# Attention in a two-block kernel: full-height score products, and one chain of products with the values per pair of heads

## The chip, the cores and the metric

The program runs on one core of a Trainium2 chip. The metric is the device time of one execution in microseconds (us), the median over runs. Engines go by short names: PE is TensorE's matmul stream, PEld its weight loads, DVE is VectorE, ACT is ScalarE, POOL is GpSimd, SP is the queue that issues the weights' DMAs.

## The reference, cut to what matters

Two blocks over 512 tokens of 1024 features, in float32. The second block has two layers. Each mixes tokens by attention with 12 heads over the tokens and 4 heads over a memory of 256 tokens, 64 features a head, and has a gated feed forward behind it. Layer 0 is causal with a forget term, layer 1 a dilated attention that the kernel writes as one softmax with a table added to the scores.

```python
# layer 0, one block of 128 queries of a head
sc = jnp.einsum('bhqd,bhkd->bhqk', qi, k, preferred_element_type=jnp.float32) * scale
sc = sc + ci[..., :, None] - c[..., None, :]
sc = jnp.where(kpos[None, :] <= qpos[:, None], sc, NEG)
p = jax.nn.softmax(sc, axis=-1)
return jnp.einsum('bhqk,bhkd->bhqd', p.astype(v.dtype), v)
# memory, both layers
p = jax.nn.softmax(sc, axis=-1)
return jnp.einsum('bhqk,bhkd->bhqd', p.astype(vm.dtype), vm)
```

## The kernel before, in words

Activations lie by features, [128 features, 512 tokens]. A float32 product is made of exact halves: an operand is split into an upper part hi in the rounded format fp32r and the rest lo, and a projection (`proj`, `mm3`, line 174) is three products of 128x512 for each of eight tiles of the contraction: hi by hi, hi by lo, lo by hi. `wload` (lines 142 to 155) loads a weight slab, and splits it on ACT (L152) and DVE (L153).

A layer's attention is `_mix` (line 1405). It handles two pairs of memory heads (256 keys) and then six pairs of heads over the tokens. A pair has 64 + 64 features on the 128 partitions, head 0 on the partitions 0 to 63 and head 1 on 64 to 127; `H` names the two ranges. For a pair the projections give q and k (48 products of 128x512), `_stack_q` and `_stack_k` make the halves, and `_attend` (line 1295) does the rest. `_stack_q` puts a head's upper half of q on its own partitions and the lower half on the other 64, in one tile `sq` per head. `_stack_k` puts the upper half of k on both ranges (`skh`, one tile per head), and the lower half of both heads into one tile `skl`, each on its own range.

`_attend` goes through two halves of the queries, and in each through two heads and two blocks of 128 queries, eight score tiles in all. A score tile has w columns: 256 for the memory; for the tokens 256, 256, 384 and 512 as the causal range grows. It takes two products: L1311 with all 128 rows (upper q and lower q by upper k), L1312 with 64 rows (upper q by lower k). In layer 0 a third, bf16 product adds the causal mask (L1314). Then comes the softmax on DVE (L1318, or L1321 and L1322) and ACT (L1319 or L1323), a scale (L1326, L1328), transposes on PE (L1331), and copies into the tile `pt` (L1334, L1336). At the end of each half the products with the values (L1340) follow: 128 rows, 64 columns of weights, head 0 into the partitions 0 to 63 of `po` and head 1 into 64 to 127. Each is recorded as two matmuls, because the operands are plain float32. `po` is split (L161, L163) and goes into the output projection `w_out_2`.

The order of the instructions on each engine is set by a scheduler when the program is built; it interleaves the projections of a later pair with the attention of an earlier one. Within an engine the order is then fixed. The tags in `_layer` (line 1557) give the buffers: `st=8` for sq, skh and skl, `pt2=2`, `pt4=1`; in PSUM `mm=3`, `sm=2` for scores, `pT=2`, `po=1`.

Of the kernel before, what the change touches and what calls it, by code (L numbers as in the profile page):

```python
# [28 lines left out]
# k-tiles of the layers' down products, in the parts that follow one another  # L29
# [3 lines left out]
# columns of the table of per-feature vectors, [128, columns]  # L33
# [11 lines left out]
# column tiles of w_in, in the order in which they are used  # L45
A_ORDER = (6, 2, 0, 4, 3, 1, 5)
# the tile of them that the modulation's shift comes in after
SHIFT_AT = 5
# pieces of the merges before the recurrence, and for each of its stages
# [7 lines left out]
def _constants():  # L57
    """Arrays that depend on shapes alone."""
    c = {}
# [33 lines left out]
class _Core:  # L93
    """Pools, constants and the pieces that every stage uses."""
# [13 lines left out]
    # ---- tiles  # L108
    @contextmanager
    def tags(self, space=None, side=None, **n):  # L110
        """Within it g(), or ps(), takes tiles of each of these tags: n of them, 2 KB a partition each."""
# [29 lines left out]
    # ---- weights: exact halves of a slab [128, kt, cols]  # L141
    def wload(self, src, kt, cols, tag=None):
        """The halves stay in tiles of a tag if one is given."""
# [13 lines left out]
    def split(self, src, tag, scale=1.0, n=512):  # L157
        """Exact halves of scale * src; scale is a power of two or a column."""
# [10 lines left out]
    def mm3(self, out, w, x, first=True, last=True):  # L169
        """out += w.T @ x for operands in exact halves: lists over the tiles of the contraction."""  # L170
        n, total = 0, 3 * len(w)
        for (wh, wl), (xh, xl) in zip(w, x):
            for a, b in ((wh, xh), (wh, xl), (wl, xh)):
                self.nc.tensor.matmul(out, lhsT=a, rhs=b, start=first and n == 0, stop=last and n == total - 1)  # L174
                n += 1

    def proj(self, src, x, kt=8, name="mm", w=None):
        """One tile [128 columns, tokens] of a product with a slab of 128 columns."""
# [7 lines left out]
    # ---- numerics on small tiles  # L186
    def rsqrt(self, y, x, t):
        """y = x ** -0.5 to float32's accuracy, for x > 0."""
# [8 lines left out]
    def exp(self, out, x, pool, shape, tag):  # L197
        """out = exp(x) to float32's accuracy; x is overwritten."""
# [15 lines left out]
    def sincos(self, sn, cs, x, pool, shape, tag):  # L214
        """Sine and cosine to float32's accuracy; x is overwritten."""
# [27 lines left out]
    def gelu2(self, out, ps, tag, n=512):  # L243
        """out = 2 gelu(ps), the tanh form."""
# [10 lines left out]
    # ---- root mean squares of a residual in tiles [128 features, tokens]  # L255
    def squares(self, xs, gain=None, tag="rm"):
        """Sums of squares over the tiles, with a gain by features."""
# [9 lines left out]
    def means(self, acc, nb=4, eps=EPS):  # L267
        """Means over the features plus eps, as columns [128 tokens, nb]."""
# [15 lines left out]
    def rms(self, xs, name):  # L284
        """Factors of the norm: columns [128 tokens, 4] and the same along the free axis, [128, 512]."""
# [35 lines left out]
# ---------------------------------------------------------------- first block  # L321


def _dot(K, raw, src, row, out, scale=1.0, after=None):
    """out = the sums over the features of src, [128 columns, features], times a row that lies on all partitions."""
# [5 lines left out]
def _ada(K, cols, tag=None, after=None):  # L331
    """Columns of silu(c) @ ada_w + ada_b into modv, 128 features each; yields after each."""
# [12 lines left out]
def _row(K, col, halves):  # L345
    """A vector of features in columns as a row, on all partitions, in two halves."""
# [8 lines left out]
def _load(K, name, rows, tag):  # L355
    """Tiles [128 features, tokens] of an array that is laid out so."""
# [8 lines left out]
def _start(K):  # L365
    """x, and h = norm(x) (1 + sc) without the norm's factors: they are left to the products."""
# [32 lines left out]
def _start_shift(K, x, g1, rs):  # L399
    """h = norm(x) (1 + sc) + sh, by features."""  # L400
# [15 lines left out]
def _memory(K):  # L416
    """The memory by features, and its norm's factors."""
# [21 lines left out]
def _mem_halves(K, l, mem, tag):  # L439
    """The memory times a layer's gain, in halves by features."""  # L440
# [14 lines left out]
def _mem_kv(K, l, mh):  # L455
    """Keys by features and values by tokens of the memory, for layer l of the second block, into DRAM."""
# [21 lines left out]
def _head_rsqrt(K, sq, scale, eps, guard, name):  # L478
    """rsqrt over the sums of sq by heads, [128, 512] in PSUM."""
# [20 lines left out]
def _wkv(K, i, la, r2, k2, v2, ya):  # L500
    """Two heads of the delta rule with decay, in chunks of 64 tokens; the output by features, in halves, goes to ya.

    Yields between its stages."""
# [4 lines left out]
    def heads(name, src):  # L508
        """Sums over the heads' features."""
# [7 lines left out]
    # decay, in-context rate, gate  # L517
# [31 lines left out]
    # normalised removal key  # L549
# [7 lines left out]
    # key  # L557
# [3 lines left out]
    # the bonus of the current token  # L561
# [6 lines left out]
    # the decayed operands  # L568
# [14 lines left out]
    # by tokens  # L583
# [21 lines left out]
    # products of the operands within a chunk, [earlier token, later token]  # L605
# [13 lines left out]
    # (1 - A)^-1 and its transpose by doubling the blocks  # L619
# [37 lines left out]
    # P = M A~ and Q = M (A_ak V)  # L657
# [30 lines left out]
    # the state over the chunks  # L688
# [23 lines left out]
    # norm over the heads, bonus, gate  # L712
# [17 lines left out]
def _wkv_consts(K, pool, la):  # L730
# [8 lines left out]
    # halves of the loras' weights: high, low, high and 32 rows of the gate's high; the gate's high, low; inputs to match  # L739
# [26 lines left out]
def _rwkv(K, x, g1, rs):  # L766
    """The columns of the recurrent branch, without the norm's factors and what the modulation's shift adds."""
# [13 lines left out]
def _rwkv_shift(K, ps, rs):  # L781
    """p + (previous p - p) mu along the tokens, with p = ps rs and what the modulation's shift adds."""
# [31 lines left out]
def _merge(K, b, outs, acc, ada, halves=None):  # L814
    """acc += 2 sigmoid(gate) y over the eight tiles of features; acc is twice the merged branches.

    Yields between its pieces."""
# [395 lines left out]
def _feed_forward(K):  # L1213
# [48 lines left out]
    return x, r2, rs2  # L1262


# --------------------------------------------------------------- second block


H = (slice(0, 64), slice(64, 128))
# [392 lines left out]
```

## Time and profile before

| what | value |
|---|---|
| median of 3 runs | 2203.45 us (2198.66 to 2204.91) |
| profiled execution: its time from the first to the last instruction (span) | 2201.7 us |
| PE busy | 2153.3 us (98%) |
| DVE busy | 1399.9 us (64%) |
| ACT busy | 937.8 us (43%) |
| PE's share of the chain that ended last | 89% |
| products of scores, rows L1311 and L1312 | 128 and 128 |
| products with the values, row L1340 | 288 + 64 records |

Of the profiled execution no other time is given than this span; the median of the runs is 1.75 us above it. The end of a PE instruction is modelled, and PE instructions overlap, so the busy time of one says little. What it costs is read from the timeline, as the distance from its start to the start of the next.

### The profile page before, as it was taken

The page shows a single profiled execution, that of the slowest core. Times are in us where ns is not written, and L with a number is a line of the kernel's source. Part 1 is how long each engine was busy: PE and PEld are TensorE (multiplying, and loading weights), DVE is VectorE, ACT ScalarE, POOL GpSimd, SP SyncE. Part 2 cuts the span into 40 slices and gives each one's busy share as a digit, 9 for nine tenths or more (in the row PEclk, how much of TensorE's full clock was granted, in tenths as well). Part 3 has the DMA queues.
Part 4 walks back from the last instruction along what each step waited for, and adds up shares of the span by engine and source line. Part 5 has one row for each costly group of instructions (what it writes and reads, how often), then busy time and mean ns, then how long its engine had stood idle before and what let it go on. Part 6 is the DMA issues. An engine that isn't in the chain of part 4 may idle for free.

```text
span 2201.7 us, 29511 instructions
## 1 busy us (share of the span) xinstructions
PE 2153.3 (98%) x11502; PEld 1703.0 (77%) x11502; DVE 1399.9 (64%) x2623; ACT 937.8 (43%) x1549; POOL 23.3 (1%) x44
## 2 busy tenths in 40 slices
PE   6999999999999999999999999999999999999998
PEld 4877787878888888886668888888866678888887
DVE  7997875555634434656656756647467767575775
ACT  3334433334423224446654423324368854242443
POOL 0010000000000000000000000000000000000000
PEclk9999999999999999999999999999999999999999
DMA  8355441133322222321212222222311122323222
GB/s 321 107 186 191 139 134 58 50 110 120 115 96 96 96 93 90 129 93 57 63 44 96 96 96 96 96 96 78 127 58 39 47 79 79 103 84 108 94 74 72
DMA packets 68091, 220.47 MB, mean 100 GB/s; under 512 B 8068, under 2 KB 11060, under 8 KB 67952
## 3 DMA queue, kind: packets, MB, share of 16 engines
q1 hardware_dynamic: 64704, 210.19, 28.0%
q0 software_dynamic: 2096, 6.30, 0.9%
q8 instruction: 91, 1.49, 0.3%
q10 hardware_dynamic: 1152, 2.10, 0.3%
q14 instruction: 48, 0.39, 0.1%
HBM read 215.25 MB, written 3.30 MB: 99 GB/s over the span
## 4 chain that ended last, share of the span: by engine, by line
PE 89%; DVE 6%; DMA 3%; ACT 1%; issue 1%; DVEq 0%; ACTq 0%; SPq 0%; POOLq 0%
PE mm L174 64%; PE gp L174 6%; PE vt L174 3%; PE po L1340 3%; PE s L1312 2%; PE yp L174 2%; DMA raw<-ada_w 2%; PE pT L1331 2%; PE s L1311 1%; DVE wlo L153 1%; PE fin L174 1%; DVE raw L328 1%; PE pu L637 0%; PE pmt L643 0%; DVE ada_w L328 0%
## 5 line engine op out<-in xcount | busy, mean ns | idle before, releaser
L174 PE MATMUL mm<-hi,whi 128*128 128x512 f32 x2088 | 831.9, 399 | 18.1 <-ACT hi L161 17.2
L174 PE MATMUL mm<-hi,wlo 128*128 128x512 f32 x2088 | 831.8, 399 | 1.0 <-DVE wlo L153 1.0
L174 PE MATMUL mm<-lo,whi 128*128 128x512 f32 x2088 | 831.8, 399 | 1.0 <-DVE lo L1227 0.5
L152 ACT ACTIVATE whi<-raw 128x1024 fp32r<-128x1024 f32 (+3 forms) x341 | 350.5, 1030 | 761.8 <-PE mm L174 611.7
L153 DVE TENSOR_TENSOR wlo<-raw,whi 128x1024 fp32r<-128x1024 f32 (+3 forms) x341 | 403.7, 1186 | 180.0 <-ACT whi L152 167.9
L174 PEld LDWEIGHTS mm<-hi,whi 128*128 128x128 f32 x2088 | 394.7, 189 | 113.8 <-ACT hi L161 20.0
L174 PEld LDWEIGHTS mm<-lo,whi 128*128 128x128 f32 x2088 | 394.3, 189 | 96.5 <-issue 4.4
L174 PEld LDWEIGHTS mm<-hi,wlo 128*128 128x128 f32 x2088 | 394.2, 189 | 95.0 <-issue 3.9
L1511 DVE TENSOR_TENSOR u<-mm,spr 128x512 f32<-128x512 f32 x88 | 60.5, 688 | 82.5 <-PE mm L174 82.2
L174 PE MATMUL gp<-hi,wlo 128*128 128x512 f32 x256 | 102.0, 399 | 3.8 <-DVE wlo L153 3.8
L174 PE MATMUL gp<-hi,whi 128*128 128x512 f32 x256 | 103.3, 404 | 0.9 <-ACT whi L152 0.9
L174 PE MATMUL gp<-lo,whi 128*128 128x512 f32 x256 | 102.3, 400 | 0.0
L1531 DVE TENSOR_TENSOR x<-x,mm 128x512 f32<-128x512 f32 x48 | 33.0, 687 | 95.8 <-PE mm L174 95.8
L1240 DVE SCALAR_TENSOR_TENSOR x<-mm,modv,x 128x512 f32<-128x512 f32 x32 | 24.0, 751 | 91.1 <-PE mm L174 91.1
L1512 ACT ACTIVATE cv<-u,vecs 128x512 f32<-128x512 f32 x88 | 71.3, 810 | 2.9 <-DVE u L1511 2.9
L1514 DVE SCALAR_TENSOR_TENSOR cv<-u,vecs,cv 128x510 f32<-128x510 f32 x88 | 66.0, 750 | 3.1
L1513 DVE SCALAR_TENSOR_TENSOR cv<-u,vecs,cv 128x511 f32<-128x511 f32 x88 | 65.6, 745 | 2.1 <-ACT cv L1512 1.8
L1522 ACT ACTIVATE cth<-cv 128x512 f32<-128x512 f32 x44 | 27.8, 632 | 86.5 <-DVE cv L1514 86.5
L1336 DVE COPY pt<-pT 128x128 f32<-128x128 f32 (+2 forms) x64 | 30.1, 473 | 51.7 <-PE pT L1331 51.7
L1319 ACT ACTIVATE p<-p,at_m 128x128 f32<-128x128 f32 (+1 forms) x96 | 53.8, 561 | 17.4 <-DVE at_m L1318 13.2
L174 PEld LDWEIGHTS gp<-hi,wlo 128*128 128x128 f32 x256 | 48.1, 188 | 16.0 <-DVE wlo L153 5.6
L174 PEld LDWEIGHTS gp<-hi,whi 128*128 128x128 f32 x256 | 48.2, 188 | 13.2 <-ACT whi L152 1.8
(532 smaller groups left out, 2647.8 us busy)
## 6 DMA issues: line engine op xcount, KB each, us to landing
raw<-w_up SPq DMA_DIRECT2D x88, 512.0 KB, 3.3
raw<-ffn_w SPq DMA_DIRECT2D x64, 512.0 KB, 3.2
raw<-w_in SPq DMA_DIRECT2D x49, 512.0 KB, 3.4
raw<-ada_w SPq DMA_DIRECT2D x32, 512.0 KB, 4.3
raw<-w_down SPq DMA_DIRECT2D x32, 384.0 KB, 3.0
ada_w<-ada_w SPq DMA_DIRECT2D x16, 512.0 KB, 8.3
raw<-w_out SPq DMA_DIRECT2D x16, 512.0 KB, 3.2
raw<-w_down SPq DMA_DIRECT2D x16, 512.0 KB, 3.2
```

The lines of the kernel that those rows point to most:

```text
L152: nc.scalar.activation(hi[:, :n], raw[:, :n], AF.Copy)
L153: nc.vector.tensor_tensor(lo[:, :n], raw[:, :n], hi[:, :n].bitcast(F32), OP.subtract)
L174: self.nc.tensor.matmul(out, lhsT=a, rhs=b, start=first and n == 0, stop=last and n == total - 1)
L1312: T.matmul(ps[:, 0:w], lhsT=q[h][H[h], c], rhs=kl[H[h], 0:w], start=False, stop=diag is None)
L1319: A.activation(p[:, 0:n], p[:, 0:n], AF.Exp, bias=nm, scale=-1.0, accum_out=l)
L1331: T.transpose(pp[:, b * 128:(b + 1) * 128], p[:, b * 128:(b + 1) * 128], K.ident)
L1340: T.matmul(po[hs, (2 * half + q0) * 128:(2 * half + 2) * 128], lhsT=vals(b, h), rhs=pt[:, h, b, q0:2], start=b == 0, stop=b == nkb - 1)
L1511: V.tensor_tensor(u, ps, rs, OP.mult)
L1512: A.activation(c, u, AF.Identity, bias=K.vec("conv_b_2", l * 44 + j), scale=tap(2))
L1513: V.scalar_tensor_tensor(c[:, 1:], u[:, 0:S - 1], tap(1), c[:, 1:], OP.mult, OP.add)
L1514: V.scalar_tensor_tensor(c[:, 2:], u[:, 0:S - 2], tap(0), c[:, 2:], OP.mult, OP.add)
L1531: V.tensor_tensor(K.xr[m], K.xr[m], ps, OP.add)
```

## The change

`_stack_k` makes the lower half of k like the upper: one tile per head, on both ranges of partitions. The second score product then takes all 128 rows of `sq` and of that tile, so it also adds lower q by lower k. The products with the values leave the loop over the halves: they come after both, second half first, the two heads in turn (1, 0), and `issue_after` puts each behind the one before it on PE. Comments are dropped, and line numbers behind `_stack_k` are higher by up to 10.

```diff
 def _stack_k(K, k, n=512):
     nc = K.nc
-    his, lo = [], K.g("skl", "st", F32R)
+    his, los = [], []
     for h in range(2):
-        hi = K.g("skh", "st", F32R)
+        hi, lo = K.g("skh", "st", F32R), K.g("skl", "st", F32R)
         for x in (h, 1 - h):
             nc.scalar.activation(hi[H[x], :n], k[H[h]], AF.Copy)
-        nc.vector.tensor_tensor(lo[H[h], :n], k[H[h]], hi[H[h], :n].bitcast(F32), OP.subtract)
+        for x in (h, 1 - h):
+            nc.vector.tensor_tensor(lo[H[x], :n], k[H[h]], hi[H[h], :n].bitcast(F32), OP.subtract)
         his.append(hi)
-    return his, lo
+        los.append(lo)
+    return his, los
...
     kh, kl = k
+    pts = []
     for half in range(2):
...
+        pts.append((pt, nkb))
...
-                T.matmul(ps[:, 0:w], lhsT=q[h][H[h], c], rhs=kl[H[h], 0:w], start=False, stop=diag is None)
+                T.matmul(ps[:, 0:w], lhsT=q[h][:, c], rhs=kl[h][:, 0:w], start=False, stop=diag is None)
...
+    last = None
+    for half in (1, 0):
+        pt, nkb = pts[half]
         for b in range(nkb):
             q0 = max(b - 2 * half, 0) if nk is None else 0
-            for h, hs in enumerate(H):
-                T.matmul(po[hs, (2 * half + q0) * 128:(2 * half + 2) * 128], lhsT=vals(b, h), rhs=pt[:, h, b, q0:2],
-                         start=b == 0, stop=b == nkb - 1)
+            for h in (1, 0):
+                with K.tc.issue_after(last) if last is not None else nullcontext():
+                    T.matmul(po[H[h], (2 * half + q0) * 128:(2 * half + 2) * 128], lhsT=vals(b, h),
+                             rhs=pt[:, h, b, q0:2], start=b == 0, stop=b == nkb - 1)
+                last = nc.cur_bb.bb.instructions[-1]
     return po
```

On PE, before, the second half of layer 0's first pair over the tokens. A row says line, operation, what is written and read, and the size; pT are the transposes, po the products with the values, mm the projections of a later pair.

```order
L1340 MATMUL po<-pt,v 64x256
L174 MATMUL mm<-hi,whi 128x512
L1331 MATMUL pT<-k_ident,p 128x128 x3
...
L1331 MATMUL pT<-k_ident,p 128x128 x4
L174 MATMUL mm<-hi,whi 128x512
L174 MATMUL mm<-lo,whi 128x512
L174 MATMUL mm<-hi,wlo 128x512
L174 MATMUL mm<-hi,whi 128x512
L1340 MATMUL po<-pt,v 64x256 x5
L1340 MATMUL po<-pt,v 64x128 x2
```

And now the end of the same pair, with the first scores of the next pair behind it:

```order
L1336 MATMUL pT<-k_ident,p 128x128 x4
L174 MATMUL mm<-lo,whi 128x512
L174 MATMUL mm<-hi,wlo 128x512
L174 MATMUL mm<-hi,whi 128x512
L174 MATMUL mm<-lo,whi 128x512
L1349 MATMUL po<-pt,v 64x256 x6
L1349 MATMUL po<-pt,v 64x128 x2
L1349 MATMUL po<-pt,v 64x256 x2
L1349 MATMUL po<-pt,v 64x128 x2
L1316 MATMUL s<-skh,sq 128x256
L1317 MATMUL s<-skl,sq 128x256
```

Before, a pair's twelve products with the values stood at four places (one alone, three, one alone, seven); for the memory eight at four places (one, three, one, three). Now they stand at one place, and the same four projection products precede it.

On DVE, before, where the lower halves of k (`skl`) of layer 0's first pair over the tokens stand among the memory heads' softmax (at_m is a row's maximum, at_l its sum):

```order
L1322 TENSOR_SCALAR at_m<-at_m 128x1
L1290 TENSOR_TENSOR skl<-qk,skh 64x512
L1321 TENSOR_REDUCE at_m<-s 128x1
L1290 TENSOR_TENSOR skl<-qk,skh 64x512
L1336 COPY pt<-pT 128x2x128
L1324 RECIPROCAL at_l<-at_l 128x1
```

And now:

```order
L1327 TENSOR_SCALAR at_m<-at_m 128x1 x2
L1291 TENSOR_TENSOR skl<-qk,skh 64x512
L1341 COPY pt<-pT 128x2x128
L1329 RECIPROCAL at_l<-at_l 128x1
L1291 TENSOR_TENSOR skl<-qk,skh 64x512
L1331 TENSOR_SCALAR p<-p,at_l 128x256
L1329 RECIPROCAL at_l<-at_l 128x1
L1291 TENSOR_TENSOR skl<-qk,skh 64x512 x2
L1323 ISA p,at_m<-s,cn 128x128
```

Two subtractions of 64x512 became four, in the same queue; two of them now stand right ahead of the first maximum over the pair's scores (L1323, before L1318).

## Rows read from the trace of the kernel before

**Rows 1.** Windows view: stretch, length, then busy us (count) of each engine, PEclk.
```profile
984.00:1152.00 168.00, 167.93 (x815) 107.69 (x814) 104.35 (x313) 105.30 (x250) 6.97 (x13) 1.00 0.18 57
1605.00:1787.00 182.00, 181.89 (x835) 118.81 (x834) 124.26 (x346) 136.63 (x307) 0.00 (x0) 1.00 0.12 42
1005.00:1020.00 15.00, 15.00 (x74) 9.59 (x74) 9.82 (x34) 11.12 (x31) 0.00 (x0) 1.00 0.11 37
1059.50:1106.40 46.90, 46.88 (x231) 30.45 (x231) 29.30 (x82) 29.21 (x66) 2.15 (x4) 1.00 0.22 68
1671.60:1718.60 47.00, 47.00 (x219) 30.46 (x220) 33.14 (x91) 37.87 (x82) 0.00 (x0) 1.00 0.13 45
```

**Rows 2.** One line's instructions: count, duration ns, forms (second score product; values).
```profile
L1312 PE MATMUL s<-skl,sq x128: 275/382/502, 984.4 to 1775.7; 64*128 64x256 f32 x80, 64*128 64x384 f32 x24, 64*128 64x512 f32 x24
L1340 PE MATMUL po<-pt,v x288: 272/379/431, 1024.4 to 1784.5; 128*64 128x256 f32 x96, 128*64 128x128 f32 x48
```

**Rows 3.** PE's timeline (start us, busy us), a score tile of 256 columns.
```profile
1616.74 0.28 PE L1311 MATMUL s<-skh,sq 128*128 128x256 f32 x1
1616.95 0.38 PE L1312 MATMUL s<-skl,sq 64*128 64x256 f32 x1
1617.26 0.50 PE L174 MATMUL mm<-hi,wlo 128*128 128x512 f32 x1
1617.60 0.39 PE L174 MATMUL mm<-hi,whi 128*128 128x512 f32 x1
1617.83 0.39 PE L174 MATMUL mm<-lo,whi 128*128 128x512 f32 x1
```

**Rows 4.** PE's timeline, two of a stream of full-height products with 256 columns.
```profile
2180.16 0.28 PE L174 MATMUL fin<-lo,whi 128*128 128x256 f32 x1
2180.28 0.28 PE L174 MATMUL fin<-hi,wlo 128*128 128x256 f32 x1
```

**Rows 5.** PE's timeline, a single product with the values, then a 384-column tile.
```profile
1680.66 0.65 PE L1340 MATMUL po<-pt,v 128*64 128x256 f32 x2
...
1681.57 0.33 PE L1311 MATMUL s<-skh,sq 128*128 128x384 f32 x1
1681.83 0.44 PE L1312 MATMUL s<-skl,sq 64*128 64x384 f32 x1
1682.20 0.50 PE L174 MATMUL mm<-lo,whi 128*128 128x512 f32 x1
```

**Rows 6.** PE's timeline, a 512-column tile in layer 0, then three products with values.
```profile
1048.48 0.48 PE L1311 MATMUL s<-skh,sq 128*128 128x512 f32 x1
1048.89 0.50 PE L1312 MATMUL s<-skl,sq 64*128 64x512 f32 x1
1049.32 0.23 PE L1314 MATMUL s<-k_causal,k_identb 128*128 128x128 bf16 x1
...
1049.76 0.86 PE L1340 MATMUL po<-pt,v 128*64 128x256 f32 x6
```

**Rows 7.** PE's timeline, three products with the memory's values in six records.
```profile
1643.58 1.08 PE L1340 MATMUL po<-pt,mv 128*64 128x256 f32 x6
```

**Rows 8.** PE's timeline, the last pair's seven products with values, in fourteen records.
```profile
1782.75 0.40 PE L174 MATMUL mm<-hi,wlo 128*128 128x512 f32 x1
1783.09 1.71 PE L1340 MATMUL po<-pt,v 128*64 128x256 f32 x14
1784.73 0.50 PE L174 MATMUL mm<-hi,whi 128*128 128x512 f32 x1
1785.07 0.39 PE L174 MATMUL mm<-lo,whi 128*128 128x512 f32 x1
```

**Rows 9.** One line's instructions on DVE: count, ns min/median/max, span, form.
```profile
L1277 DVE TENSOR_TENSOR sq<-qk,sq x32: 684/686/689, 975.3 to 1757.2; 64x512 fp32r<-64x512 f32 x32
L1290 DVE TENSOR_TENSOR skl<-qk,skh x24: 673/687/691, 1010.9 to 1767.2; 64x512 fp32r<-64x512 f32 x24
```

**Rows 10.** Weight loads of the first score product, and ACT's split of po.
```profile
L1311 PEld LDWEIGHTS s<-skh,sq x128: 186/188/247, 984.1 to 1775.3; 128*128 128x128 f32 x128
L161 ACT ACTIVATE hi<-po x16: 597/598/601, 1005.0 to 1784.8; 128x512 fp32r<-128x512 f32 x16
```

## Prediction

> **What bounds the kernel now.** I read the page first: PE is busy 98% of the span and has 89% of the chain that ended last. The change touches only the two attention stages, so the windows view was cut to them. In layer 0's stage PE is busy 167.93 of 168.00 us, in layer 1's 181.89 of 182.00, at a granted clock of 1.00 throughout, while DVE has 104.35 and 124.26, ACT 105.30 and 136.63 [rows 1]. Time that PE gives back there is therefore worth something until DVE or ACT become the limit. By pairs: two token pairs take 46.90 us in layer 0 (DVE 29.30, ACT 29.21), two take 47.00 in layer 1 (DVE 33.14, ACT 37.87); a memory pair takes some 15.0 (DVE 9.82, ACT 11.12) [rows 1].
>
> Busy PE is not PE at its pace, so the timeline was read for starts. Two full 128x512 products start 0.23 us apart (1617.60, 1617.83) [rows 3]. A full-height product of 256 columns takes 0.12 [rows 4]. A score tile of 256 columns, whose second product uses 64 rows, takes 0.21 to its second product and 0.31 more to what follows, 0.52 in all; the projection's next product then comes after 0.34 instead of 0.23 [rows 3]. So each turn from 128 rows to 64 and back costs more than the product itself.
>
> **First edit: the second score product at full height.** There are 128 of them: 80 with 256 columns, 24 with 384, 24 with 512 [rows 2]. If it takes the pace of a full-height product, a tile of 256 falls from 0.52 to 2 x 0.12 = 0.24, gain 0.28. With 384: 0.63 before (1681.57 to 1682.20 [rows 5]); two products at 0.17, half way between 0.12 and 0.23, make 0.35 (rounded up), gain 0.28. With 512: 0.84 (1048.48 to 1049.32 [rows 6]) against 2 x 0.23, gain 0.38. The late next product, 0.34 - 0.23 = 0.11, is saved where a projection's product stands right behind the 64-row one, at 59 places in the order before (memory pairs and layer 1; in layer 0 the mask's product stands between). Sum: 80 x 0.28 + 24 x 0.28 + 24 x 0.38 + 59 x 0.11 = 22.4 + 6.7 + 9.1 + 6.5 = 44.7 us of PE.
>
> Here a rule speaks against the change. The rows first: a full 128x128 weight load of the score product takes 188 ns [rows 10], longer than the 0.12 between 256-column products, so in that stream the loads lie under the products before them. The Trainium skill, page "TensorE: Matmul & The Clock Gate", section "Part 3: Packing small matmuls — row/col tiling", says that a weight load overlaps a running matmul only when it goes to other row groups of the array. By that rule every second score product, now of all rows, would wait for its load; [rows 4] don't agree with it.
>
> **Second edit: the chain of products with the values.** A single product (two records) is recorded as 0.65, six records as 1.08, fourteen as 1.71 [rows 5, 7, 8]. Six records are three products, two of them of different heads side by side; so the two further products' worth costs 1.08 - 0.65 = 0.43, the price of one slot of 256 columns, whether one head or both are in it. Fourteen records, seven products, in 1.71 say the same. A slot of 128 columns is half of it, 0.22. Around a chain: the first product starts 0.34 after a projection's, the second projection's product behind it 0.34 after the first (1782.75 to 1783.09, 1784.73 to 1785.07 [rows 8]), against 0.23 each, so 0.22; and the next start lies 0.07 before the recorded end. A place with one product thus costs 0.65 - 0.07 + 0.22 = 0.80; with three of a token pair 0.86 - 0.07 + 0.22 = 1.01 [rows 6]; with three of the memory 1.23 [rows 7]; with seven 1.86 [rows 8].
>
> A token pair before: 2 x 0.80 + 1.01 + 1.86 = 4.47. After: four slots of 256 and two of 128 with both heads in each, 4 x 0.43 + 2 x 0.22 = 2.16; the first slot's start 0.65 - 0.43 - 0.07 = 0.15; around it 0.22; 2.53. Gain 1.94, for 12 pairs 23.3. A memory pair before: 2 x 0.80 + 2 x 1.23 = 4.06; after 4 x 0.43 + 0.15 + 0.22 = 2.09; gain 1.97, for four 7.9. Together 31.2 us of PE.
>
> PE's sum is 44.7 + 31.2 = 76 us, the upper bound of the gain: per token pair 4.4 in layer 0 (four tiles x 0.28, two x 0.28, two x 0.38, 1.94), 5.0 in layer 1 (0.65 for late products besides), 4.9 per memory pair.
>
> **What is added.** Two subtractions of 64x512 per token pair on DVE. They cross partitions as L1277 does, 686 ns against 687 for L1290 in its own place [rows 9]: 1.37 us per pair, half of that columns for the memory (taken as 0.8). Twelve pairs and four: 16.4 + 3.2 = 20 us of DVE, hidden while DVE idles. Queued behind them is the maximum over the pair's first scores, for which ACT's exponentials and then PE's transposes wait. No DMA and no queue of SP or POOL is moved.
>
> **What is left over the new floors.** Layer 0: PE 23.45 - 4.4 = 19.05 a pair, DVE 14.65 + 1.37 = 16.0. DVE is at 84% of the period and everything on PE waits for it in turn, so I let one sixth of the gain go: 3.7 x 6 = 22. Layer 1: PE 18.5, ACT 18.9, DVE 16.6 + 1.4 = 18.0: the ceiling is ACT's, gain 4.6, and three engines so close to each other wait for each other; I take two thirds, 3.1 x 6 = 18.4. Memory pair: PE 10.1, ACT 11.1, DVE 10.6; ceiling 3.9, two thirds 2.6 x 4 = 10.4. The shares are my choice; no row has a stage with three engines over 90%. At the end of layer 1 the output projection's products on the last pair's heads stand right behind the chain, where four products (0.92) stood before; they wait for ACT's split of `po`, 0.60 [rows 10]: 1 us lost. Sum: 22 + 18.4 + 10.4 - 1 = 50 us.
>
> The profiled span is 2201.7; the median of the runs is 1.75 above. The gain is taken off the median: 2203.45 - 50 = **2153 us**. A measurement can tell about 0.3%, 6.6 us, from no change.
>
> **Rivals.**
> 1. PE stays the bound throughout, nearly all of the 76 us arrive: 2127. For it: PE never idles now, and the interleaving is as dense as before. Against: the floors of layer 1. Over 65 us of gain: 0.15.
> 2. DVE and ACT become the bound. Layer 1's ACT is busy 37.87 of 47.00 [rows 1] with PE pacing it; should it not get closer to full than about 85%, a pair takes 22.3 and gains 1.2, a memory pair 1.5, a layer 0 pair 2: 7 + 6 + 12 = 25, 2178; lower still if the order fits badly, down to 7. The chain not running the heads side by side ends here too: 2.16 x 12 + 1.72 x 4 = 33 us of PE back. Chance 0.18.
> 3. The full-height weight load isn't hidden: 128 x 0.188 = 24 us of PE back, 1.5 a pair. Layer 0 then gains 2.9, five sixths 2.4 x 6; layer 1 3.5, two thirds 2.3 x 6; memory 3.4, 2.3 x 4: 37, 2166. That is the Trainium skill's rule of above at work. Chance 0.06, since [rows 4] speak against it.
> 4. Slower: the buffers of `st`. A pair held five of eight, now six, so the next pair's last tiles of k wait for this pair's last scores, and then for ACT's two copies and DVE's two subtractions of about 0.69, some 3 us. After a pair's last scores PE has some sixteen projection products (0.23 each) and the chain (2.5), 6.2 us, so this is covered; it decides only if the wait passes 6.2 + 4.4 = 10.6 us a pair. At 12 us: 12 x 1.4 = 17 slower, 2220. Chance 0.03.
> 5. Nothing measurable, gains and new waits cancel: 0.03.
>
> **Chances.** Forecast (gain 30 to 65) 0.55, rivals 0.15, 0.18, 0.06, 0.03, 0.03. Faster by over 0.3%: 0.55 + 0.15 + 0.18 + 0.06 = 0.94; same 0.03; slower 0.03. The range runs from 2130, most of rival 1, to 2182, the better part of rival 2.
>
> **What would show it.** Right: L1312's successor L1317 with 128 rows, about 0.12 from L1316's start for 256 columns; 24 records of values in one place in about 2.4 us; PE idle in layer 1, waiting for ACT and DVE, little in layer 0; token pairs near 19.8 and 20.4 us; the projections elsewhere unchanged. Wrong: steps of 0.3 around L1317 (rival 3), 24 records in over 4 us, or pairs in layer 1 still at 23 us. The prediction fails altogether if PE's waits in the stages pass 70 us.

## The result, and the profile after

The changed kernel takes 2148.64 us (median of 4 runs, 2145.07 to 2149.26), the kernel before, timed beside it, 2203.07 (4 runs). The ratio is 0.9751, with a 95% interval of 0.9739 to 0.9763: faster by 54.4 us, where 50 was forecast. Its profiled execution has a span of 2147.4 us, 54.3 less than before.

The page of the changed kernel, the busy times of the span and the chain that ended last:

```profile
PE 2094.6 (98%) x11502; PEld 1692.7 (79%) x11502; DVE 1416.1 (66%) x2655; ACT 934.1 (43%) x1549; POOL 23.5 (1%) x44
...
PE 85%; DVE 6%; ACT 4%; DMA 2%; issue 1%; DVEq 0%; ACTq 0%; SPq 0%
```

PE is still at 98% and still has most of the chain; over the whole span nothing seems to have changed but the length. The stages say more. The windows view of the changed kernel (columns as in [rows 1]): the two attention stages, then two token pairs of layer 0 and two of layer 1.

```profile
984.00:1127.00 143.00, 142.63 (x845) 106.09 (x844) 112.60 (x328) 103.52 (x253) 6.95 (x13) 1.00 0.22 70
1580.00:1733.00 153.00, 147.45 (x821) 108.80 (x821) 128.01 (x357) 134.08 (x302) 0.00 (x0) 1.00 0.14 47
1047.80:1087.40 39.60, 39.58 (x233) 30.01 (x234) 31.71 (x87) 28.55 (x67) 2.15 (x4) 1.00 0.26 81
1656.70:1696.40 39.70, 38.19 (x216) 28.48 (x217) 35.18 (x96) 38.07 (x82) 0.00 (x0) 1.00 0.16 54
```

Against [rows 1], a token pair has gone from 23.45 to 19.80 us in layer 0 and from 23.5 to 19.85 in layer 1. The two numbers are alike, their causes are not. In layer 0 PE is busy 39.58 of 39.60 us and ACT 28.55. In layer 1 PE idles for 1.51 us in two pairs, and ACT is busy 38.07 of 39.70: PE no longer seems to be what paces this stage; the experiments below ask that. Over the stages PE idles 0.37 us in layer 0 and 5.55 in layer 1, against 0.07 and 0.11 before [rows 1]. PE's waits in layer 1's stage, by what ended them (sum, times, longest; the three largest):

```profile
PE pT L1336 <- ACT p L1333: 2.1, 5, 0.7
PE mm L174 <- ACT hi L161: 0.7, 1, 0.7
PE s L1316 <- DVE at_m L1323: 0.6, 1, 0.6
```

The first is the transposes waiting for ACT's scale of the probabilities. The second is the wait foreseen at the end of the layer, the output projection for the split of `po`: 0.7 us.

How long a stage is can be read from ACT's split of `po` (L161), which follows each pair's chain of values: eight in each layer, with the first and the last start in the row. Before:

```profile
L161 ACT ACTIVATE hi<-po x8: 597/598/601, 1005.0 to 1152.6; 128x512 fp32r<-128x512 f32 x8
L161 ACT ACTIVATE hi<-po x8: 597/598/600, 1629.0 to 1784.8; 128x512 fp32r<-128x512 f32 x8
```

And after:

```profile
L161 ACT ACTIVATE hi<-po x8: 594/598/599, 1002.4 to 1125.2; 128x512 fp32r<-128x512 f32 x8
L161 ACT ACTIVATE hi<-po x8: 597/598/599, 1597.5 to 1730.5; 128x512 fp32r<-128x512 f32 x8
```

From the first split to the last, layer 0 went from 147.6 to 122.8 us, layer 1 from 155.8 to 133.0. The last split of layer 0 comes 27.4 us earlier than before, that of layer 1 54.3 earlier, and what follows it takes 417 us in both kernels. So 27.4 us were gained up to the end of layer 0 and 26.9 from there to the end of layer 1. Nearly all of that lies in the two stages: from a layer's first score product to its last split, layer 0 is 28.5 us shorter (168.5 to 140.0) and layer 1 24.8 (176.2 to 151.4).

The lines that [rows 2] and [rows 9] showed of before:

```profile
L1317 PE MATMUL s<-skl,sq x128: 274/283/481, 985.5 to 1721.7; 128*128 128x256 f32 x80, 128*128 128x384 f32 x24, 128*128 128x512 f32 x24
L1349 PE MATMUL po<-pt,v x288: 272/379/432, 1030.2 to 1730.1; 128*64 128x256 f32 x96, 128*64 128x128 f32 x48
L1291 DVE TENSOR_TENSOR skl<-qk,skh x48: 666/685/690, 1009.4 to 1714.6; 64x512 fp32r<-64x512 f32 x48
```

The second score product has 128 rows in all 128 places, the products with the values are as many as before and not shorter, and the added subtractions cost what the old ones did. What changed on PE is the distance between starts. PE's timeline of the changed kernel (start, busy time): the end of a pair of layer 1, its chain of values, and the next pair's first scores.

```profile
1691.58 0.40 PE L174 MATMUL mm<-hi,wlo 128*128 128x512 f32 x1
1691.92 2.38 PE L1349 MATMUL po<-pt,v 128*64 128x256 f32 x24
1694.24 0.38 PE L1316 MATMUL s<-skh,sq 128*128 128x256 f32 x1
1694.46 0.28 PE L1317 MATMUL s<-skl,sq 128*128 128x256 f32 x1
1694.58 0.28 PE L1316 MATMUL s<-skh,sq 128*128 128x256 f32 x1
1694.69 0.28 PE L1317 MATMUL s<-skl,sq 128*128 128x256 f32 x1
1694.81 0.39 PE L174 MATMUL mm<-hi,whi 128*128 128x512 f32 x1
```

All 24 records of the pair's values take 2.38 us, start to next start 2.32. The chain begins 0.34 after the projection's product, as before. The scores behind it go at 0.12, 0.11, 0.12, as the stream of [rows 4] did; only the step from the first of them is 0.22. The same is seen at a tile that begins after a short wait (0.38 instead of 0.23 behind the product ahead of it), and at one of 512 columns behind transposes:

```profile
1677.05 0.40 PE L174 MATMUL mm<-lo,whi 128*128 128x512 f32 x1
1677.43 0.36 PE L1316 MATMUL s<-skh,sq 128*128 128x256 f32 x1
1677.62 0.28 PE L1317 MATMUL s<-skl,sq 128*128 128x256 f32 x1
1677.74 0.40 PE L174 MATMUL mm<-hi,wlo 128*128 128x512 f32 x1
...
1682.79 0.44 PE L1336 MATMUL pT<-k_ident,p 128*128 128x128 f32 x2
1682.98 0.48 PE L1316 MATMUL s<-skh,sq 128*128 128x512 f32 x1
1683.29 0.39 PE L1317 MATMUL s<-skl,sq 128*128 128x512 f32 x1
1683.52 0.39 PE L174 MATMUL mm<-hi,whi 128*128 128x512 f32 x1
```

The first product's step is 0.19 instead of 0.12 in the one, 0.31 instead of 0.23 in the other; the second product's step is 0.12 and 0.23, the full pace. The forecast had taken the full pace for both.

Why a step is late can be read in part from PEld's timeline, the weight loads. In the kernel before, at the tile of [rows 3], the load of the 64-row product begins when the product does (1616.95), and so does the load of the projection's product behind it (1617.26):

```profile
1616.95 0.18 PEld L1312 LDWEIGHTS s<-skl,sq 64*128 64x128 f32 x1 [0.25 <-issue]
1617.26 0.19 PEld L174 LDWEIGHTS mm<-hi,wlo 128*128 128x128 f32 x1
```

It is so, within 0.003 us, for 125 of the 128 64-row products. In the changed kernel the load of the second product begins at least 0.1 us ahead of it, while the product before runs, in 107 of 128 tiles. At the tile behind the chain only the first product (1694.24 above) starts together with its own load, and it is the one whose step is late:

```profile
1694.23 0.19 PEld L1316 LDWEIGHTS s<-skh,sq 128*128 128x128 f32 x1 [0.17 <-ACT skh L1289]
1694.34 0.19 PEld L1317 LDWEIGHTS s<-skl,sq 128*128 128x128 f32 x1
```

Of the 160 score products of 256 columns, the 97 whose load begins at least 0.1 us ahead have a step of 0.12 us at the median, the 55 whose load begins less than 0.06 ahead one of 0.20. So most second products now have their load under the product before, which three of 128 had before the change. What keeps a load from running ahead behind another shape or type is not shown.

### The profile page after: what moved, and what is told of

Its sections match the earlier page's. It is cut to its first block, busy times and chain, and to the rows that moved or that the text cites. A ratio compares the mean times of both kernels' runs of the same rounds, so it can differ in the third digit from the quotient of the medians.

```text
span 2147.4 us, 29518 instructions
## 1 busy us (share of the span) xinstructions
PE 2094.6 (98%) x11502; PEld 1692.7 (79%) x11502; DVE 1416.1 (66%) x2655; ACT 934.1 (43%) x1549; POOL 23.5 (1%) x44
## 4 chain that ended last, share of the span: by engine, by line
PE 85%; DVE 6%; ACT 4%; DMA 2%; issue 1%; DVEq 0%; ACTq 0%; SPq 0%
PE mm L174 62%; PE gp L174 7%; PE vt L174 3%; PE yp L174 2%; DMA raw<-ada_w 2%; PE pT L1336 1%; DVE wlo L153 1%; PE po L1349 1%; PE fin L174 1%; PE s L1316 1%; PE s L1317 1%; ACT whi L152 1%; DVE raw L328 1%; ACT p L1324 1%; PE pmt L643 1%
## 5 line engine op out<-in xcount | busy, mean ns | idle before, releaser
L153 DVE TENSOR_TENSOR wlo<-raw,whi 128x1024 fp32r<-128x1024 f32 (+3 forms) x341 | 403.5, 1186 | 180.2 <-ACT whi L152 170.7
L174 PEld LDWEIGHTS gp<-lo,whi 128*128 128x128 f32 x256 | 48.6, 190 | 10.6 <-issue 0.4
```

Source lines behind the costliest of these rows:

```text
L153: nc.vector.tensor_tensor(lo[:, :n], raw[:, :n], hi[:, :n].bitcast(F32), OP.subtract)
```

## The experiments

In each diff the minus lines are the changed kernel's. Kernels timed at different times stand beside different medians of before, so they are compared by their ratios to before: a difference of 0.001 is 2.2 us. "The changed kernel" is at 0.9751.

**Each edit alone.** `e1_scores` keeps the full-height scores and puts the products with the values back after each half:

```diff
-    last = None
-    for half in (1, 0):
-        pt, nkb = pts[half]
...
+            for h, hs in enumerate(H):
+                T.matmul(po[hs, (2 * half + q0) * 128:(2 * half + 2) * 128], lhsT=vals(b, h), rhs=pt[:, h, b, q0:2],
+                         start=b == 0, stop=b == nkb - 1)
```

> Score part alone (full-height second score product, two more subtractions per pair; products with the values as before, at 64 places). Theory (each turn of the array's shape has its own price, and ACT paces the middle of layer 1 in the changed kernel): PE's steps fall by the 31 us that L1316 and L1317 fell between the two traces, so 28 to 36 us faster than before, 2167 to 2175; together with the chain alone more than the 54.4 us of both, because the last microseconds of both meet ACT's limit. Rival, strictly additive: the two parts sum to 54.4. Rival, only the chain matters: within 7 us of before.

Measured: 2167.60 us against 2202.14, ratio 0.9842 (0.9825 to 0.9859), 34.5 us faster than before. `e2_chain` keeps the chain and goes back to 64 rows:

```diff
-        for x in (h, 1 - h):
-            nc.vector.tensor_tensor(lo[H[x], :n], k[H[h]], hi[H[h], :n].bitcast(F32), OP.subtract)
+        nc.vector.tensor_tensor(lo[H[h], :n], k[H[h]], hi[H[h], :n].bitcast(F32), OP.subtract)
...
-                T.matmul(ps[:, 0:w], lhsT=q[h][:, c], rhs=kl[h][:, 0:w], start=False, stop=diag is None)
+                T.matmul(ps[:, 0:w], lhsT=q[h][H[h], c], rhs=kl[H[h], 0:w], start=False, stop=diag is None)
```

> Chain alone (one place per pair, heads in turn; second score product with 64 rows as before, no added work on DVE). Theory: 48 places fewer and all heads side by side, priced at 31 us of PE, of which the values' own steps fell by 20 between the two traces: 24 to 32 us faster than before, 2171 to 2179. Rival, only the scores matter: within 7 us of before.

Measured: 2177.48, ratio 0.9895 (0.9872 to 0.9919), 24.7 us faster than before. Both edits pay, the scores more. Together they give 54.4, not the sum of 59.2; the intervals of the three ratios are too wide for a difference of 5 us, but the profiled executions show one and where it lies. From a layer's first score product to its last split of `po`, the scores alone take 15.8 us off layer 0, the chain alone 12.3, and both together 28.5, the sum. Off layer 1 they take 20.1 and 10.1, and together 24.8, five less than the sum. The second layer comes to an end of what PE's savings can buy.

**The heads in turn.** `e3_serial` keeps one chain per pair, but with all products of head 1 ahead of those of head 0:

```diff
-    for half in (1, 0):
-        pt, nkb = pts[half]
-        for b in range(nkb):
-            q0 = max(b - 2 * half, 0) if nk is None else 0
-            for h in (1, 0):
+    for h in (1, 0):
+        for half in (1, 0):
+            pt, nkb = pts[half]
+            for b in range(nkb):
+                q0 = max(b - 2 * half, 0) if nk is None else 0
```

> The changed kernel with its chain still at one place, but all products of head 1 before all of head 0. Theory (two heads run side by side): each token pair loses 2.16 us and each memory pair 1.72, 33 us of PE; 24 to 33 us slower than the changed kernel, 2173 to 2182. Rival (the gain comes from fewer places alone): no more than 3 us slower, 2146 to 2152.

Measured: 2170.70, ratio 0.9851 (0.9836 to 0.9865), 22 us slower than the changed kernel, a little less than the 24 expected at the least. PE's timeline of this kernel, a pair's chain and what follows (the granted clock is 1.00 here too):

```profile
1069.89 3.95 PE L1349 MATMUL po<-pt,v 128*64 128x256 f32 x24
1073.77 0.50 PE L174 MATMUL mm<-hi,wlo 128*128 128x512 f32 x1
```

The same 24 records take 3.95 instead of 2.38 us: 1.57 more a pair, 18.8 for the twelve token pairs. From each start to the next, without waits, all products with the values take 57.75 us here and 35.35 in the changed kernel; the difference, 22.4, is as much as the whole loss. So two products of different heads do run side by side when they stand next to each other, and this, not the one place by itself, is most of what the chain is worth. They do not run for nothing: five slots of 256 columns take (2.32 - 0.15) / 5 = 0.43 us each with two heads in them, ten with one head (3.88 - 0.15) / 10 = 0.37, where 0.15 is the first slot's start as in the prediction. The prediction and the expectation had put one price on both, which is why the loss came out smaller.

**One place or two.** `e4_halves` ends the order at each half, so that a chain stands behind each half's tiles:

```diff
-    last = None
     for half in (1, 0):
...
+        last = None
```

> The changed kernel with a chain at the end of each half, heads in turn: 32 places instead of 16. Theory: a place costs 0.37 us on PE (0.22 around, 0.15 at its start), so 6 us slower than the changed kernel, 2151 to 2157. Rival (holding the first half's values back makes PE wait at the chain or keeps buffers): equal or faster, 2142 to 2149.

Measured: 2151.76, ratio 0.9769 (0.9751 to 0.9786), some 4 us slower than the changed kernel, though the two intervals overlap. By the prediction's prices a second place costs 0.15 + 0.22 = 0.37 us, 16 x 0.37 = 6. In the profiled execution the products with the values take 37.70 us instead of 35.35, 0.147 for each of the 16 places more. From the first score product to the last split the layers are 1.0 and 1.6 us longer, while PE idles 1.8 us less in them: 4.4 us of PE's time in all. So a place has a price, roughly the forecast one, and some of it was hidden in waits that PE had anyway.

**Which engine paces which layer.** `e10_act_l1` does each copy of k's upper half twice in layer 1's token pairs, with the same result; `e11_act_l0` does it in layer 0's:

```diff
-        for x in (h, 1 - h):
+        for x in (h, 1 - h) * (2 if n == 512 and K.lay == 1 else 1):
             nc.scalar.activation(hi[H[x], :n], k[H[h]], AF.Copy)
```

> In layer 1's token pairs each copy of k's upper half is done twice on ACT, with the same result: 4 x 0.63 = 2.5 us a pair, 15 us in all. Theory, layer 1 is paced by ACT and DVE (ACT 19.03 of 19.85 us a pair): a pair takes at least 21.5, so 10 to 15 us slower than the changed kernel, 2159 to 2164. Rival, PE paces it in spite of its idle time: 2149 to 2153.

> The same copies done twice in layer 0's token pairs instead: ACT 14.3 + 2.5 = 16.8 of 19.8 us a pair. Theory, layer 0 is paced by PE (39.58 busy of 39.60): 2149 to 2153. Rival, work queued ahead of the scores counts in full on any engine that they wait for: 2159 to 2164.

Measured: 2159.84, ratio 0.9808 (0.9792 to 0.9823), for layer 1; 2149.41, ratio 0.9758 (0.9743 to 0.9774), for layer 0. The same 15 us of ACT cost 12.6 us in one layer and nothing that can be told apart from none in the other. ACT's split of `po`, first with the copies in layer 1:

```profile
L161 ACT ACTIVATE hi<-po x8: 585/597/598, 999.9 to 1122.8; 128x512 fp32r<-128x512 f32 x8
L161 ACT ACTIVATE hi<-po x8: 597/597/602, 1597.7 to 1742.6; 128x512 fp32r<-128x512 f32 x8
```

then in layer 0:

```profile
L161 ACT ACTIVATE hi<-po x8: 573/597/600, 1002.6 to 1126.6; 128x512 fp32r<-128x512 f32 x8
L161 ACT ACTIVATE hi<-po x8: 597/598/600, 1596.9 to 1729.9; 128x512 fp32r<-128x512 f32 x8
```

Layer 1 grew from 133.0 to 144.9 us, layer 0 from 122.8 to 124.0, and in each run the other layer kept its length within 0.1 us. `e8_dve2` asks the same of DVE, in both layers at once: the four subtractions are done twice.

```diff
         for x in (h, 1 - h):
             nc.vector.tensor_tensor(lo[H[x], :n], k[H[h]], hi[H[h], :n].bitcast(F32), OP.subtract)
+        for x in (h, 1 - h):
+            nc.vector.tensor_tensor(lo[H[x], :n], k[H[h]], hi[H[h], :n].bitcast(F32), OP.subtract)
```

> The changed kernel with each pair's four subtractions for the lower half of k done twice on DVE (the second time with the same result): 2.75 us more per token pair, 1.7 per memory pair, 40 us more of DVE. Theory (DVE has slack in layer 0 and little in layer 1): layer 0 hides nearly all, layer 1 shows about half of its 20: 8 to 16 us slower, 2157 to 2165. Rival (DVE paces both layers): 25 to 40 us slower. Rival (hidden everywhere): within 4 us.

Measured: 2163.71, ratio 0.9818 (0.9792 to 0.9845), some 15 us slower. Each layer has 20 us more of DVE (24 x 0.685 + 8 x 0.42); between the splits layer 0 grew by 2.6 us and layer 1 by 12.7. So layer 0 is paced by PE and hides most of such work, and layer 1 is paced by ACT and DVE, both of them. Part of layer 1's loss in `e10_act_l1` and `e8_dve2` has another cause, PE's clock, which the last section shows.

**Can layer 1 be relieved?** `e9_scale_dve` moves two of ACT's four scales of a layer 1 token pair to DVE:

```diff
-                if (qb + h) % 2:
+                if (qb + h) % 2 or (nk is None and diag is None and qb < 2):
                     V.tensor_scalar(p[:, 0:n], p[:, 0:n], l, None, OP.mult)
```

> Layer 1's token pairs alone: two of ACT's four scales per pair (128 and 256 columns, 0.40 and 0.50 us on ACT) go to DVE (0.28 and 0.35). ACT falls from 19.03 to 18.1 us a pair, DVE rises from 17.6 to 18.2, PE's own work is 19.1. Theory A, ACT alone paces layer 1: up to 0.75 us a pair, 2144.5 to 2147. Theory B, ACT and DVE take turns and what counts is their sum (36.6 of 39.7 us per two pairs each): next to nothing, 2147.5 to 2150. Rival, DVE is the tighter of the two: 2151 or more.

Measured: 2149.14, ratio 0.9753 (0.9739 to 0.9766): theory B. The windows view of this kernel, 80 us of layer 1:

```profile
1640.00:1720.00 80.00, 77.15 (x433) 57.73 (x432) 71.81 (x195) 69.27 (x154) 0.00 (x0) 1.00 0.16 54
```

and of the changed kernel:

```profile
1640.00:1720.00 80.00, 76.70 (x429) 56.34 (x429) 70.85 (x188) 73.43 (x162) 0.00 (x0) 1.00 0.16 54
```

ACT fell from 73.43 to 69.27 us, DVE rose by 1.0, PE's busy time by 0.45, and nothing came of it. PE now waits less for ACT's scale (1.5 us in the stage instead of 2.1) and more for DVE's maxima (1.3 instead of 0.6).

Three runs asked whether POOL, nearly idle, can take some of it. `e5_pool` gives it the subtraction onto the other head's partitions, `e6_scale_pool` all of ACT's scales, `e12_wlo_pool` (on top of `e9_scale_dve`) the lower half of one of a pair's two weight slabs in layer 1:

```diff
-        for x in (h, 1 - h):
-            nc.vector.tensor_tensor(lo[H[x], :n], k[H[h]], hi[H[h], :n].bitcast(F32), OP.subtract)
+        nc.vector.tensor_tensor(lo[H[h], :n], k[H[h]], hi[H[h], :n].bitcast(F32), OP.subtract)
+        nc.gpsimd.tensor_tensor(lo[H[1 - h], :n], k[H[h]], hi[H[h], :n].bitcast(F32), OP.subtract)
```

> The changed kernel with the second of each head's two subtractions on POOL instead of DVE; it takes the change's 20 us off DVE. Theory (ACT paces layer 1, DVE's added work is hidden): within 3 us of the changed kernel, 2145 to 2152. Rival (DVE's added work paces layer 1, its share of the 20 us is 10): 4 to 10 us faster, 2139 to 2145. If POOL needs much more than DVE's 0.69 us for it, the score products wait for it and it is slower.

```diff
-                    A.activation(p[:, 0:n], p[:, 0:n], AF.Copy, scale=l)
+                    nc.gpsimd.tensor_scalar(p[:, 0:n], p[:, 0:n], l, None, OP.mult)
```

> The changed kernel with ACT's half of the softmax scales (8 of 16 per two heads and pair, L1333, 0.56 us each) on POOL. Theory (ACT paces the middle of layer 1, with 38 of 39.7 us busy over two pairs): ACT loses 2.2 us per pair, six pairs in layer 1 get up to 2 us shorter each: 4 to 10 us faster, 2139 to 2145. Rival (PE or DVE paces): within 3 us. If POOL is much slower than ACT, its latency shows in the transposes and the kernel gets slower.

```diff
-        nc.vector.tensor_tensor(lo[:, :n], raw[:, :n], hi[:, :n].bitcast(F32), OP.subtract)
+        (nc.gpsimd if getattr(self, 'side', 0) else nc.vector).tensor_tensor(lo[:, :n], raw[:, :n], hi[:, :n].bitcast(F32), OP.subtract)
...
-        q, k = feature_tile(i, l == 1), feature_tile(6 + i, l == 1)
+        q = feature_tile(i, l == 1)
+        K.side = l == 1
+        k = feature_tile(6 + i, l == 1)
+        K.side = 0
```

> As the one before, and POOL makes the lower half of one of a pair's two weight slabs in layer 1 (1.21 us on DVE; on POOL an estimated 3.3, twice the 1.63 that 64x512 took there). Weights are fetched ahead, so its duration may be covered, which that of k's lower halves was not. DVE 17.0, ACT 18.1, PE 19.1 a pair. Theory A or B: PE's waits in layer 1 (8 us) shrink by half or more, 2142 to 2146. Rival, POOL's duration isn't covered by the three buffers of weights: 2152 or more.

Measured: `e5_pool` 2165.59, ratio 0.9814 (0.9794 to 0.9835), 14 us slower than the changed kernel; `e6_scale_pool` 2188.31, ratio 0.9923 (0.99 to 0.9946), 38 slower; `e12_wlo_pool` 2152.69, ratio 0.978 (0.9761 to 0.9799), 6 slower. None of them helped, and each missed what its theory expected. In `e6_scale_pool` the cause is plain: PE waited 35.6 us for POOL's scales, which took 1.09 us each at the median where ACT took 0.51. In the other two PE hardly waited for POOL itself (1.1 us in `e5_pool`, nothing in layer 1 of `e12_wlo_pool`), so the rival expected for `e12_wlo_pool` is not what slowed it; the cause is told in the last section.

**The buffers.** `e7_st10` gives layer 1 ten buffers of `st` instead of eight:

```diff
-    with K.tags(ao=16, p=3, pt2=2, pt4=1, cn=2 if l else 4, v=1, mkv=2, st=8, **({"dil": 1} if l else {})):
+    with K.tags(ao=16, p=3, pt2=2, pt4=1, cn=2 if l else 4, v=1, mkv=2, st=10 if l else 8, **({"dil": 1} if l else {})):
```

> The changed kernel with ten instead of eight buffers for the halves of q and k in layer 1. Theory (the buffers decide nothing): within 3 us of the changed kernel, 2145 to 2152. Rival (a pair's six of eight tiles hold the next pair's back): 3 to 8 us faster, 2140 to 2146.

Measured: 2149.06, ratio 0.9745 (0.9728 to 0.9762), no difference. In layer 1 the sixth tile of eight takes nothing; layer 0 was not tried. No variant beats the changed kernel.

## Why the prediction was right, and which terms were not

The time came within 5 us, the sign and the range held, and the mechanisms named were the ones that worked. The sum hides two errors that cancel, though. PE's own gain was put at 76 us, of which 26 would be lost to the other engines. What PE gained by itself is the gain of the span plus the idle time that it has taken on: 54.3 + (0.37 + 5.55 - 0.07 - 0.11) = 60.0 us, and the loss is 5.7. The terms, worked out as sums of the distances from each start on PE to the next over both stages, without the waits in them:

| term (us) | forecast | measured |
|---|---|---|
| steps of the 256 score products | 38.2 | 78.4 - 46.9 = 31.5 |
| steps of the products with the values | 20.6 | 55.85 - 35.35 = 20.5 |
| what is late around them (6.5 + 10.6) | 17.1 | the rest, 8.0 |
| PE together | 76 | 60.0 |
| lost to waits | 26 | 5.7 |
| gain of the span | 50 | 54.3 |

The middle column's 20.6 is the prediction's 31.2 without the 0.22 around each of three places that go, for 16 pairs.

- **The second score product.** Right in kind, and the forecast for the second product itself holds in most tiles: 0.12, 0.17, 0.23 for 256, 384, 512 columns. Too much by 7 us, mostly because the first product's step was taken at that pace as well. Behind transposes, behind the values, behind the mask, or after a wait it is 0.19 to 0.22 for 256 columns and 0.31 for 512 (the timeline above). Over the 128 tiles the first products' steps sum to 25.6 us and the second's to 21.3, where 19.3 each was forecast; the steps of before were 1.5 more than priced. The row used for the price, [rows 4], came from a stream of one kind of product; a score tile is two products between others.
- **Rival 3** is thereby true in a small part. It priced 128 unhidden loads of the second product at 24 us. In 107 tiles that load ran ahead, and with 256 columns the step is then 0.12, less than the load's 0.188 [rows 10]. In 20 tiles, nearly all of them behind transposes or the mask, it began within 0.04 us of the product, and the step is 0.08 to 0.09 us longer: 1.7 us in all. The late steps of the first products go with their own loads, which were there before the change too. The Trainium skill, page "TensorE: Matmul & The Clock Gate", section "Part 3: Packing small matmuls — row/col tiling", says that a weight load overlaps a running matmul only when it goes to other row groups. The 107 tiles do not agree with this as it stands: their loads go to all rows, behind products of all rows, and overlap them.
- **The chain.** 24 records were forecast at 2.31 us from the first start to the next product's regular place; the timeline shows 2.32. The heads side by side were shown by `e3_serial`; that a place has a price is borne out by `e4_halves`, at 4.4 us for sixteen places instead of 6.
- **Late products around.** Too much by 7 to 9 us. A place was charged 0.22 as if a projection's stream ran on without it; many removed places stood beside transposes, whose next product is late in any case (1681.00 to 1681.31 behind three transposes of the changed kernel). The 8.0 is only what the other terms leave. Summed directly, what the projections' products of 512 columns take beyond 0.23 us each fell from 23.8 to 15.5 us in the two stages, and the transposes' steps fell by 1.8: 10 us.
- **Layer 0.** Forecast 22 + 5.2 = 27.2, measured 27.4, by the wrong route and so by luck: five sixths of too large a gain. There was no sixth to lose, since DVE is 80% busy (31.71 of 39.60) and PE waits for it almost nowhere. `e8_dve2` and `e11_act_l0` put 20 us of DVE and 15 of ACT into this layer and lost 2.6 and 1.2.
- **Layer 1.** Forecast 18.4 + 5.2 - 1 = 22.6, measured 26.9 from the end of layer 0 to the end of layer 1, or 24.8 from the layer's first score product. The bound was named right (ACT, with DVE close behind), and `e10_act_l1` shows that it holds. The two thirds taken were too few: ACT goes to 96% before PE's waits reach 1.5 us in two pairs. Rival 2, ACT stuck near 85%, fell with that.
- **Rival 1**, PE the bound throughout, holds in layer 0 and not in layer 1. **Rival 4**, the buffers, fell with the time itself, and `e7_st10` found nothing of it in layer 1.
- **What was added** cost what was said, 0.685 us each, and its cover is there in layer 0. In layer 1 the cover is thin: in that layer the added subtractions are part of what now paces it.

## What to carry to other kernels

Price a product on PE by the distance to the next start in the surroundings in which it will stand, not by the best stream in the trace: behind a change of shape, of type or a wait the same product costs 0.07 to 0.1 us more here, and the timeline of the weight loads shows which products are hit. Products that use 64 columns of weights each, as those of two heads with the values, belong next to each other in the order: neighbours ran side by side, and head after head did not. Before spending PE's time savings, read the other engines' busy share in each stage by itself: the same edit was worth all of its PE time in one layer and stopped at ACT and DVE in the other, and there neither moving work between those two nor giving it to POOL bought anything.

## What the runs showed that was not expected

**POOL holds DVE up.** In `e5_pool` the subtractions that stayed on DVE, the same instruction as in [rows 9], took much longer:

```profile
L1290 DVE TENSOR_TENSOR skl<-qk,skh x24: 674/1655/1774, 1009.0 to 1731.9; 64x512 fp32r<-64x512 f32 x24
```

The median is 1655 ns where it was 687 [rows 9]. In `e12_wlo_pool` the weights' subtraction on DVE (L153), 1.2 us by itself, took up to 2.94:

```profile
L153 DVE TENSOR_TENSOR wlo<-raw,whi x11: 1197/1218/2944, 1584.6 to 1741.0; 128x1024 fp32r<-128x1024 f32 x11
```

Seen at one place of that kernel, POOL's timeline first:

```profile
1593.17 2.37 POOL L153 TENSOR_TENSOR wlo<-raw,whi 128x1024 fp32r<-128x1024 f32 x1 [15.75 <-ACT whi L152]
```

and DVE's:

```profile
1594.24 1.45 DVE L1331 TENSOR_SCALAR p<-p,at_l 128x256 f32<-128x256 f32 x1
1595.61 0.41 DVE L1326 TENSOR_REDUCE at_m<-s 128x1 f32<-128x256 f32 x1
...
1598.65 0.35 DVE L1331 TENSOR_SCALAR p<-p,at_l 128x256 f32<-128x256 f32 x1
```

A scale that takes 0.35 us by itself started while POOL was at work and ended at 1595.69, just after POOL did at 1595.54. Scores' reductions, copies and products that read PSUM (L1326, L1341, L1430) kept their durations in the same runs. So work given to POOL was not simply taken off DVE: where it met DVE's subtractions and scales between tiles in SBUF, it held them until it was done. The reciprocals on columns of one element (L1329) ran through beside it in their usual 0.16 us. PE felt it through DVE: in layer 1 of `e12_wlo_pool` it waited 4.8 us for DVE's maxima (L1323), against 0.6 in the changed kernel. The Trainium skill, page "SBUF — State Buffer", section "SBUF: two separate sides", says that DVE and GpSimd share a pair of ports under an exclusive lock that is held for a whole instruction, and that it concerns DVE's operations with two inputs in SBUF and those in its two-port fast modes. The traces agree for the subtractions, which have two inputs in SBUF (687 to 1655 ns), and for the scale above if it ran in such a mode, which no run here shows.

**PE's clock fell behind some of the waits.** In the kernels before and after, the granted clock is 1.00 throughout both stages. In `e10_act_l1` the windows view shows:

```profile
1672.50:1675.50 3.00, 1.17 (x9) 0.71 (x10) 1.79 (x3) 2.90 (x6) 0.00 (x0) 0.98 0.02 5
1675.50:1678.50 3.00, 3.00 (x20) 1.91 (x18) 1.76 (x3) 2.90 (x5) 0.00 (x0) 0.50 0.00 0
```

and PE's timeline in that stretch:

```profile
1672.24 0.40 PE L174 MATMUL mm<-hi,wlo 128*128 128x512 f32 x1
1673.69 0.66 PE L1336 MATMUL pT<-k_ident,p 128*128 128x128 f32 x4 [1.05 <-ACT p L1333]
1675.13 4.07 PE L1349 MATMUL po<-pt,v 128*64 128x256 f32 x24 [0.78 <-DVE pt L1341]
1679.13 0.39 PE L1316 MATMUL s<-skh,sq 128*128 128x256 f32 x1
```

PE had waited 1.05 us for ACT and 0.78 for DVE; then the clock went to its lower level, 1.2 GHz, for the pair's chain, and 24 records took 4.07 us instead of 2.38: 1.7 us lost on top of the waits. `e8_dve2` has two such stretches in layer 1, of about 3.5 and 7 us, the first behind 2 us almost without PE work:

```profile
1653.50:1655.50 2.00, 0.08 (x1) 0.08 (x1) 1.97 (x4) 1.98 (x6) 0.00 (x0) 1.00 0.01 4
1656.50:1659.50 3.00, 3.00 (x10) 2.03 (x8) 2.29 (x4) 2.90 (x6) 0.00 (x0) 0.50 0.51 162
```

`e5_pool` has one in layer 0, some 3 us long, behind waits of 0.58 and 0.82 us, which is about 1.7 us of its loss. But waits do not always bring it. In `e6_scale_pool` PE waited for POOL 50 times, once for 2.4 us, and the granted clock stayed at 1.00 throughout both stages; the wait, and 80 us of layer 1 around the longest of them:

```profile
PE pT L1336 <- POOL p L1333: 35.6, 50, 2.4
...
1640.00:1720.00 80.00, 67.61 (x369) 48.96 (x369) 61.84 (x161) 59.41 (x128) 21.21 (x15) 1.00 0.14 47
```

What decides it, these runs do not show.

So of the 12 to 13 us that `e10_act_l1` and `e8_dve2` lost in layer 1 a part is the clock's: about 1.7 in the first; in the other at most 5, from about 10 us at the lower level. The loss that is left, 8 to 10 us, still tells layer 1 from layer 0. The changed kernel itself, with waits of at most 0.7 us, did not pay this.
